# A fused diffusion block and state-space block on one core: first stage in written order, operator products on VectorE, their inputs loaded in long runs and turned on TensorE

## The chip, the cores and the metric

The kernel runs on one core of a Trainium2 chip. The metric is the device time of one execution in microseconds (us), and the time of a version is the median of its runs. A core has five engines that run side by side, each through its own row of instructions: TensorE (PE in the profile, with the weight loads as PEld), VectorE (DVE), ScalarE (ACT), GpSimd (POOL) and SyncE (SP), which issues transfers. [...] Engines wait for each other by semaphores.

## The reference

Two blocks run one behind the other on 256 tokens of width 1024, all in float32.

```python
def first_block(x, c, ctx, c_ctx, ada_w, ...):
    silu_c, silu_cc = jax.nn.silu(c), jax.nn.silu(c_ctx)
    for i in range(DEPTH):                                  # 2 layers
        mod_lat = (silu_c @ ada_w[i] + ada_b[i])[:, None, :]     # adaLN: 1024 x 6144 weights
        mod_ctx = (silu_cc @ ada_w[i] + ada_b[i])[None, None, :]
        sh1, sc1, ga1, sh2, sc2, ga2 = jnp.split(mod_lat, 6, axis=-1)
        ...
        u_lat = modulate(rms_norm(h_lat, g_mix[i]), sh1, sc1)
        u_ctx = modulate(rms_norm(h_ctx, g_mix[i]), csh1, csc1)
        # i == 0: q, k, v of both; neighbourhood attention with a bias; i == 1: sliding window
        ...
        # then h + ga1 * y, and a squared-ReLU MLP of width 4096

def s5_mixer(xn, w_in, lam_re, lam_im, b_re, b_im, c_re, c_im, d_skip, log_dt, w_glu):
    u = (xn @ w_in).astype(f32)
    lam = lax.complex(lam_re, lam_im);  dt = jnp.exp(log_dt)[:, None]
    a_bar = jnp.exp(lam * dt)
    b_bar = ((a_bar - 1.0) / lam)[..., None] * b_mat        # 64 groups, 64 states, 16 inputs
    # scan  s = a_bar * s + b_bar u,  y = Re(c s) + d_skip * u, in chunks
    ...
    val, gate = jnp.split(jax.nn.gelu(y) @ w_glu, 2, axis=-1)
    return val * jax.nn.sigmoid(gate)

def second_block(x, ...):
    # s5_mixer, conv FFN, stick-breaking attention, conv FFN, each with a residual
    ...
```

The operators of the state-space layer hang on weights alone (lambda, dt, b, c, d). The kernel builds them at its very beginning, beside the adaLN work of the first layer, and puts them in DRAM for later.

## The kernel before

Activations lie transposed, in 8 tiles `h[k]` (tokens) and 8 tiles `hc[k]` (context) of 128 x 256: 128 of the 1024 channels by 256 tokens. A product with a weight is done in three passes of a rounded format: the weight is split in `whi` (ScalarE) and a remainder `wlo` (VectorE), the input in `xh` and `xl`, and TensorE adds whi·xh, wlo·xh and whi·xl in one PSUM bank `g` (helper lines 301 to 303, for the first attention layer's projections).

The first stage stands in lines 902 to 988. In it are:

- *Loads.* The condition vectors, the constant table `cst` (with the identity `ident`), the S5 weights (`s5_load`, line 574: `lt` for lambda, `ld` for dt, `bt` for b, `ci` for c, `dr` for d), the tokens and context (`xloads`), and about 20 small vectors (`small_loads`: into `va`, `swg` and, for the attention bias, `rp` and from there to DRAM as `rpad`). All are issued by SyncE through `dma`. `bt` is read with states on the partitions, which makes runs of 64 bytes.
- *adaLN.* 16 steps `ada_step()`, each with 512 KB of `ada_w` (issue in line 354) in buffers `ada` and `stl` and eight matmuls into a bank `x` (line 359). After eight steps the sum goes through `adacc` (a VectorE copy, then a turn on TensorE, line 366) into the modulation vectors `mods` and `scg`. `prep_vectors` turns `va` (line 213) into `vt`, which holds their biases and gains. The first projection needs the modulation of both groups of eight steps, 16 in all.
- *Turns and norm.* x and ctx are transposed on TensorE and copied to `h` and `hc` by ScalarE; `rstd` squares them (ScalarE), sums over channels (TensorE, line 427), takes the reciprocal of the root (VectorE, line 431) and spreads it over the partitions (TensorE, line 438).
- *State-space operators* (class `S5`). The constructor makes the powers of a_bar (`pw`, 0 to 8) and b_bar (`bb`). `c()` turns `ci` on TensorE, has ScalarE copy it to `ct`, and makes `dd` (d on a diagonal, 32 x 1024) on VectorE. For each r in 0 to 3, `e(r, eng)` forms the complex products of powers and b_bar: two tiles `e` from 24 instructions of 128 x 256, 16 products into `tm` and 8 sums or differences into `e`. r = 0 and 1 are on VectorE, 2 and 3 on GpSimd. `k1(r)` multiplies `e` with `cbk` (from ct) and adds dd on TensorE into one bank (lines 722 and 725), copied to `kt`; `et(r)` transposes the e tiles (line 736), which ScalarE copies to `et` and SyncE stores in DRAM as `edr` (line 739); `k2(r)` turns kt into `kst` (line 744). `zero()`, `save()` and `k_out()` store zeros, ct and the powers (`cdr`), and kst (`kdr`, line 759).
- *First projection.* `normed` makes xh and xl from h and hc, and the projections of the first attention layer begin; the heads' attention is worked in pairs, with scores `sc` (line 1106), a bias `bt` loaded from rpad (line 1088), softmax on VectorE and ScalarE, transposes `pt` of the probabilities p (line 850) and p·v into `po` (line 1120).

The order of each engine's instructions is not that of the code: a scheduler of the framework chooses among the instructions that it takes to be ready, by its own model of their costs, over the whole program. In the ordering of the first stage k1 of r = 0 thus falls between adaLN steps, and SyncE's stores of edr among its weight loads. A tile waits for its buffer to come free; a buffer is named by its tag.

Of the kernel before, what the change touches and what calls it, by code (L numbers as in the profile page):

```python
# [16 lines left out]
D = 1024  # L17
KT = 8
# [64 lines left out]
def _build(ctx, tc, I, out, dbg):  # L83
# [3 lines left out]
    dma = nc.sync.dma_start  # L87
# [82 lines left out]
    def vector_loads(va, cc):  # L170
# [31 lines left out]
        return [lambda o=o, i=i: dma(out=o, in_=i) for o, i in todo]  # L202
# [370 lines left out]
    def s5_load(pp):  # L573
# [3 lines left out]
        bt = [spare(i, f"bt{i}").rearrange("p (g h) -> p g h", h=16) for i in range(2)]  # L577
# [5 lines left out]
        for r, nm in ((0, "a_b_re_2"), (1, "a_b_im_2")):  # L583
            todo.append((bt[r], I[nm][0].rearrange("(g j) p h -> (j p) g h", j=2)))
# [4 lines left out]
        return (lt, ld, dr, bt, ci), [lambda o=o, i=i: dma(out=o, in_=i) for o, i in todo]  # L589

    class S5:


        def __init__(self, pp, loads):
# [10 lines left out]
            for i in range(4):  # L605
                T.transpose(pl[:, i * 32:(i + 1) * 32], lt[:, i, :], ident[0:32, 0:32])
            L = pp.tile([128, 128], F32, name="L")
# [23 lines left out]
            self.pw = pw = [pp.tile([128, 9, 32], F32, name=f"pw{i}") for i in range(2)]  # L631
            G.memset(pw[0][:, 0, :], 1.0)
# [17 lines left out]
            tb = [tmp_tile().rearrange("p (g h) -> p g h", h=16) for _ in range(2)]  # L650
            cmul(bb, bt, cb, tb)
# [8 lines left out]
            for r in range(2):  # L660
                act(pf[:, r], pw[r][:, 1:9, :], AF.Copy)
            u = [(cs, sn), (s_[7], s_[8])]
            for i in range(3):
                cmul((ph[:, 0], ph[:, 1]) if i == 2 else u[(i + 1) % 2], u[i % 2], u[i % 2], (t0, t1))

            self.em = [[pp.tile([128, 4, 2, 8, 16], F32, name=f"e{r}{i}") for i in range(2)] for r in range(3)]
            self.tm = [spare(2 + i, f"tm{i}").rearrange("p (i j t h) -> p i j t h", i=2, j=2, t=8) for i in range(2)]
            self.kt = [None] * 4
            self.ci, self.dr = ci, dr

        def c(self):
            pp, ct, ci, dr = self.pp, self.ct, self.ci, self.dr

            for r in range(2):
                for i in range(2):
# [3 lines left out]
                    for j in range(2):  # L679
# [3 lines left out]
            cbs = spare(5, "cbk")  # L683
            G.memset(cbs, 0.0)
            self.cbk = [cbs[:, 256 * i:256 * i + 256].rearrange("p (q a b h) -> p q a b h", q=4, a=2, b=2)
                        for i in range(2)]
# [10 lines left out]
        def save(self):  # L697
            for i in range(2):
                dma(out=cdr[:, 512 * i:512 * i + 512], in_=self.ct[i].rearrange("p g h -> p (g h)"))
# [193 lines left out]
    with ExitStack() as sa:  # L893
# [11 lines left out]
        with ExitStack() as s0:  # L905
# [28 lines left out]
            def some(n):  # L934
                for f in small_loads[0:n]:
                    f()
# [924 lines left out]
```

## Time and profile before

| | before |
|---|---|
| median of 3 runs | 1799.22 us (1796.97 to 1801.13) |
| profiled execution | 1797.98 us, span 1796.3 us |
| TensorE busy | 1712.8 us (95% of the span) |
| VectorE busy | 1177.8 us (66%) |
| ScalarE busy | 795.9 us (44%) |
| GpSimd busy | 468.4 us (26%) |
| mean granted TensorE clock | 0.983 |

The rows are from one profiled execution, the one of 1797.98 us. "Busy" is time in which an instruction runs, issuing of transfers left out. A wait is put down to the instruction whose semaphore came last. Matmul records of one engine overlap, because matmuls are pipelined: the pace of a row of matmuls is seen from their starts and not from their lengths. A float32 matmul is recorded as two passes, a transpose as one.

### The profile page before, as it was taken

How to read it: one execution, taken by the hardware profiler on the slowest of the kernel's cores; microseconds unless marked ns; L12 is line 12 of the kernel's file. 1: busy time of each engine (PE TensorE's matmuls, PEld its weight loads, DVE VectorE, ACT ScalarE, POOL GpSimd, SP SyncE). 2: the span in 40 equal slices, each digit the busy share in tenths (PEclk: the TensorE clock that was granted, in tenths of full speed). 3: DMA queues.
4: the chain of work that ended last, by engine and by line, in shares of the span. 5: the costliest groups of instructions: out<-in, count | busy, mean ns of one | idle time of the engine just before them, and what ended most of it. 6: DMA issues, size and time to landing. Idle time of an engine off the chain costs nothing. (4 is left out here: it accounts for less than half of the span.)

```text
span 1796.3 us, 33733 instructions
## 1 busy us (share of the span) xinstructions
PE 1712.8 (95%) x13161; PEld 1504.6 (84%) x13161; DVE 1177.8 (66%) x2412; ACT 795.9 (44%) x1463; POOL 468.4 (26%) x633
## 2 busy tenths in 40 slices
PE   5899999989999999999998999989999999999999
PEld 3478888867777777888877999978899999789998
DVE  7656887865535343446985656768576788958674
ACT  4354444543413132323674535536444465544443
POOL 5312221125699100030102000221431322424130
PEclk9899999999999999999999999999999999999999
DMA  8565455434666655332216666798459474335852
GB/s 216 178 175 162 138 167 160 109 104 138 199 208 210 192 158 161 93 95 82 72 35 165 177 194 182 222 294 223 129 149 244 141 220 141 107 107 165 230 150 89
DMA packets 441042, 286.57 MB, mean 160 GB/s; under 512 B 50450, under 2 KB 418610, under 8 KB 440882
## 3 DMA queue, kind: packets, MB, share of 16 engines
q1 hardware_dynamic: 439122, 278.64, 53.8%
q0 software_dynamic: 1760, 5.77, 0.8%
q8 instruction: 104, 1.70, 0.4%
q14 instruction: 56, 0.46, 0.1%
HBM read 271.41 MB, written 17.15 MB: 161 GB/s over the span
## 5 line engine op out<-in xcount | busy, mean ns | idle before, releaser
L108 ACT ACTIVATE whi<-raw 128x1024 fp32r<-128x1024 f32 (+2 forms) x388 | 389.7, 1012 | 487.9 <-PE g L294 345.8
L111 DVE TENSOR_TENSOR wlo<-raw,whi 128x1024 fp32r<-128x1024 f32 (+2 forms) x388 | 466.2, 1206 | 186.7 <-ACT whi L108 183.3
L295 PE MATMUL g<-xh,wlo 128*128 128x256 f32 (+1 forms) x1216 | 374.8, 308 | 5.5 <-DVE wlo L111 5.2
L293 PE MATMUL g<-xh,whi 128*128 128x256 f32 (+1 forms) x1216 | 374.8, 309 | 1.2 <-ACT xh L108 1.2
L294 PE MATMUL g<-xl,whi 128*128 128x256 f32 (+1 forms) x1216 | 373.9, 308 | 0.0
L293 PE MATMUL g<-oh,whi 128*128 128x256 f32 (+1 forms) x1056 | 331.5, 315 | 3.5 <-ACT oh L108 1.4
L295 PE MATMUL g<-oh,wlo 128*128 128x256 f32 (+1 forms) x1056 | 331.2, 314 | 0.0
L294 PE MATMUL g<-ol,whi 128*128 128x256 f32 (+1 forms) x1056 | 330.9, 313 | 0.0
L295 PEld LDWEIGHTS g<-xh,wlo 128*128 128x128 f32 x1216 | 234.6, 193 | 17.9 <-DVE wlo L111 7.4
L293 PEld LDWEIGHTS g<-xh,whi 128*128 128x128 f32 x1216 | 234.5, 193 | 16.6 <-ACT whi L108 3.5
L294 PEld LDWEIGHTS g<-xl,whi 128*128 128x128 f32 x1216 | 234.8, 193 | 9.6
L293 PEld LDWEIGHTS g<-oh,whi 128*128 128x128 f32 x1056 | 198.0, 188 | 23.9 <-issue 3.9
L294 PEld LDWEIGHTS g<-ol,whi 128*128 128x128 f32 x1056 | 198.3, 188 | 15.2 <-issue 0.9
L295 PEld LDWEIGHTS g<-oh,wlo 128*128 128x128 f32 x1056 | 198.3, 188 | 14.4 <-issue 0.2
L301 PE MATMUL g<-whi,xh 128*128 128x256 f32 x560 | 167.9, 300 | 3.8 <-ACT xh L108 2.8
L302 PE MATMUL g<-wlo,xh 128*128 128x256 f32 x560 | 161.9, 290 | 0.4 <-DVE wlo L111 0.4
L303 PE MATMUL g<-whi,xl 128*128 128x256 f32 x560 | 160.8, 289 | 0.1
L114 DVE SCALAR_TENSOR_TENSOR h<-g,mods,h 128x256 f32<-128x256 f32 x64 | 30.9, 483 | 140.7 <-PE g L295 140.7
L301 PEld LDWEIGHTS g<-whi,xh 128*128 128x128 f32 x560 | 108.8, 194 | 14.7 <-issue 10.3
L302 PEld LDWEIGHTS g<-wlo,xh 128*128 128x128 f32 x560 | 108.7, 194 | 2.1 <-DVE wlo L111 1.5
L303 PEld LDWEIGHTS g<-whi,xl 128*128 128x128 f32 x560 | 108.1, 194 | 1.1 <-issue 0.6
L108 ACT ACTIVATE oh<-t 128x256 fp32r<-128x256 f32 (+1 forms) x108 | 51.3, 482 | 125.5 <-DVE t L111 125.5
(304 smaller groups left out, 2873.0 us busy)
## 6 DMA issues: line engine op xcount, KB each, us to landing
raw<-mlp_w SPq DMA_DIRECT2D x128, 512.0 KB, 4.4
ada<-ada_w SPq DMA_DIRECT2D x88, 512.0 KB, 6.1
raw<-ffn_w_up SPq DMA_DIRECT2D x88, 512.0 KB, 5.5
raw<-ffn_w_down SPq DMA_DIRECT2D x32, 384.0 KB, 3.8
raw<-ffn_w_down SPq DMA_DIRECT2D x32, 320.0 KB
raw<-na_wqkv SPq DMA_DIRECT2D x32, 256.0 KB, 4.0
raw<-a_w_glu SPq DMA_DIRECT2D x16, 512.0 KB, 7.4
raw<-w_kv SPq DMA_DIRECT2D x16, 512.0 KB, 5.5
```

The costliest lines, as they stand in the source:

```text
L108: last[0] = A.activation(out=o, in_=i, func=f, **kw)
L111: (e or V).tensor_tensor(out=o, in0=a, in1=b, op=op)
L114: V.scalar_tensor_tensor(out=o, in0=a, scalar=s, in1=b, op0=op0, op1=op1)
L293: T.matmul(ps, lhsT=a, rhs=xh[k][:, s0:s1], start=first, stop=False)
L294: T.matmul(ps, lhsT=a, rhs=xl[k][:, s0:s1], start=False, stop=False)
L295: T.matmul(ps, lhsT=b, rhs=xh[k][:, s0:s1], start=False, stop=last_)
L301: T.matmul(ps, lhsT=xh[k][:, t0:t0 + 128], rhs=a, start=first, stop=False)
L302: T.matmul(ps, lhsT=xh[k][:, t0:t0 + 128], rhs=b, start=False, stop=False)
L303: T.matmul(ps, lhsT=xl[k][:, t0:t0 + 128], rhs=a, start=False, stop=last_)
```

## The change

The first stage stands in a `tc.manual_schedule` block for all five engines: there each engine runs the instructions in the order in which the code issues them, up to the operators of r = 1 and the last three adaLN steps. The code of the stage is rewritten in the order meant: S5 constructor, turns of x and ctx, power tables, four adaLN steps, c, e(0), two steps, norm and vectors, three steps, e(1), the operators of r = 0, and so on. Behind the block the scheduler decides again.

The products e(r) are all on VectorE, in 12 instructions of 128 x 512 for each r. For that, GpSimd copies the powers into `pz` (8 copies of 128 x 64) in another order, and b_bar is written in that order. b is loaded in four transfers with runs of 4 KB (32 x 1024 each), and 64 small TensorE operations (32 transposes, 32 float32 matmuls with the identity, 96 passes in all) turn it into two PSUM banks, from where VectorE multiplies it.

The small vector loads, rpad and the four ci loads are issued by GpSimd; the S5 loads besides ci, and the stores of et, ct and the powers, by ScalarE. k1 issues four matmuls that write to four groups of 32 partitions behind one another, and the dd matmuls in two groups of four. The copies of the powers for `pf` come in `c()`. The pool `pp` is allocated from the other side of the memory.

```diff
-        bt = [spare(i, f"bt{i}").rearrange("p (g h) -> p g h", h=16) for i in range(2)]
+        bt = [[pp.tile([128, 1024], F32, tag=f"e{1 + r}{j}", name=f"bt{r}{j}")[0:32] for j in range(2)]
+              for r in range(2)]
...
-            todo.append((bt[r], I[nm][0].rearrange("(g j) p h -> (j p) g h", j=2)))
+            for j in range(2):
+                todo.append((bt[r][j], I[nm][0].rearrange("(g j) p h -> g j (p h)", j=2)[:, j]))
...
-        return (lt, ld, dr, bt, ci), [lambda o=o, i=i: dma(out=o, in_=i) for o, i in todo]
+        return (lt, ld, dr, bt, ci), [
+            lambda o=o, i=i, n=n: (G.dma_start if 7 <= n < 11 else dma_a)(out=o, in_=i) for n, (o, i) in enumerate(todo)]
...
+            pb = [bank("s") for _ in range(2)]
+            for r in range(2):
+                for j in range(2):
+                    b_ = bt[r][j].rearrange("g (p h) -> g h p", h=16)
+                    for h_ in range(16):
+                        o_ = pb[r][64 * j:64 * j + 64, 32 * h_:32 * h_ + 32]
+                        if j:
+                            T.matmul(o_, lhsT=b_[:, h_, :], rhs=ident[0:32, 0:32])
+                        else:
+                            T.transpose(o_, b_[:, h_, :], ident[0:32, 0:32])
...
+            self.pw2 = [pp.tile([128, 32, 8], F32, name=f"pz{i}") for i in range(2)]
+            for i in range(2):
+                for r in range(4):
+                    ts(self.pw2[i][:, 8 * r:8 * r + 8, :].rearrange("p (q j) t -> p q j t", q=4),
+                       pw[i][:, 0:8, :].rearrange("p t (q r j) -> p r q j t", q=4, r=4)[:, r], 1.0, MUL, 0.0, ADD, e=G)
...
-        def e(self, r, eng):
-            em, tm = self.em[r], [self.tm[eng is G][:, i] for i in range(2)]
...
-            for q in range(4):
-                cmul([x_[:, q] for x_ in em], [x_[:, q].unsqueeze(3).to_broadcast([128, 2, 8, 16]) for x_ in pa],
-                     [x_[:, q].unsqueeze(2).to_broadcast([128, 2, 8, 16]) for x_ in ma], tm, e=eng)
+        def e(self, r):
+            for hf in range(2):
+                g = slice(8 * r + 4 * hf, 8 * r + 4 * hf + 4)
+                cmul([x_.rearrange("p q j t h -> p (q j) t h")[:, 4 * hf:4 * hf + 4] for x_ in self.em[r]],
+                     [x_[:, g, :].unsqueeze(3).to_broadcast([128, 4, 8, 16]) for x_ in self.pw2],
+                     [x_[:, g, :].unsqueeze(2).to_broadcast([128, 4, 8, 16]) for x_ in self.bb], self.tm)
...
-            for q in range(4):
-                for jp in range(2):
-                    for i in range(2):
+            for jp in range(2):
+                for i in range(2):
+                    for q in range(4):
                         T.matmul(kp[32 * q:32 * q + 32, jp * 128:(jp + 1) * 128],
...
+                for q in range(4):
                     T.matmul(kp[32 * q:32 * q + 32, jp * 128:jp * 128 + 16], lhsT=self.dd[:, 8 * q + 2 * r + jp, :],
...
-                dma(out=edr[:, 16 * q + 4 * r:16 * q + 4 * r + 4, :], in_=et)
+                dma_a(out=edr[:, 16 * q + 4 * r:16 * q + 4 * r + 4, :], in_=et)
...
-            s5.e(0, V)
-            s5.e(2, G)
...
+            with tc.manual_schedule(engines={ENG.PE, ENG.DVE, ENG.Activation, ENG.SP, ENG.Pool}):
+                for f in vloads[0:2] + [lambda: dma(out=cst, in_=I["cst"])] + sloads[0:7] + xloads + small_loads[0:15]:
+                    f()
+                prep_cond(cc, sc)
+                s5 = S5(pp, loads)
...
+                s5.tables()
...
+                ada(4)
+                s5.c()
+                s5.e(0)
+                ada(2)
+                act(small, h[KT - 2][:, 0:1], AF.Sqrt, bias=eps, scale=0.0)
+                r_ = rstd(512, 0, None, "s")
+                prep_vectors(va)
+                ada(3)
+                s5.e(1)
+                operators(0)
+                ada(2)
+                w_first = [Weights(wpairs(w, D, 0), by_k=True)]
+                ada(2)
+                s5.e(2)
+                small_loads[-1]()
...
+                operators(1)
+                ada(3)
+            w_first.append(Weights(wcols(w, 2 * D, 256), by_k=True))
+            x = new_x(xa, "x", 512)
+            normed(x, r_, 512, lambda k, v: scg[0][:, 0, k, v:v + 1], lambda k, v: modcol(0, 0, k, v))
+            operators(2)
+            s5.e(3)
+            operators(3)
```

How this moves instructions is seen in the row of each engine. On TensorE, behind the spread of the reciprocal root, before the change (`e_268` and `e_269` are the two e tiles of r = 0):

```order
L438 MATMUL s<-sd,cst 128x128 x4
L359 MATMUL x<-ada,sl 32x256 x4
L722 MATMUL s<-e_268,cbk 32x128
L722 MATMUL s<-e_269,cbk 32x128
L736 MATMUL s<-cst,e_268 128x128 x2
L725 MATMUL s<-cst,dd 32x16
L722 MATMUL s<-e_268,cbk 32x128
L722 MATMUL s<-e_269,cbk 32x128
L213 MATMUL x<-cst,va 128x128
L725 MATMUL s<-cst,dd 32x16
```

and after it (`e_426` and `e_427` are the same two tiles):

```order
L367 MATMUL x<-cst,adacc 128x128 x2
L360 MATMUL x<-ada,sl 32x256 x4
L751 MATMUL s<-e_426,cbk 32x128 x4
L751 MATMUL s<-e_427,cbk 32x128 x4
L755 MATMUL s<-cst,dd 32x16 x4
L751 MATMUL s<-e_426,cbk 32x128 x4
L751 MATMUL s<-e_427,cbk 32x128 x4
L755 MATMUL s<-cst,dd 32x16 x4
L766 MATMUL s<-cst,e_426 128x128 x2
```

k1 of r = 0 now comes behind the first adaLN accumulator and in one piece, with four matmuls of one shape behind one another, where pieces of other steps stood among the matmuls before.

On VectorE, at the end of the first products, before the change:

```order
L111 TENSOR_TENSOR tm_274<-pw_200,bb_221 128x256
L431 RECIPROCAL sd<-sd 128x128
L111 TENSOR_TENSOR e_268<-tm_274 128x256
L111 TENSOR_TENSOR tm_274<-pw_199,bb_221 128x256
L111 TENSOR_TENSOR tm_274<-pw_200,bb_220 128x256
L111 TENSOR_TENSOR dd<-dr,cst 32x1024
L111 TENSOR_TENSOR e_269<-tm_274 128x256
```

and after it, at their beginning (`ph` is the last of the power tables):

```order
L112 TENSOR_TENSOR ph<-sm 128x32
L112 TENSOR_TENSOR dd<-dr,cst 32x1024
L112 TENSOR_TENSOR tm_432<-pz_398,bb_309 128x512
L112 TENSOR_TENSOR tm_433<-pz_399,bb_310 128x512
L112 TENSOR_TENSOR e_426<-tm_432,tm_433 128x512
```

dd has moved from among the last products of r = 0 to ahead of the first.

On TensorE, at the first pair of attention heads (`q_1300`, and after it `q_1335`, is the query of that pair), before the change:

```order
L359 MATMUL x<-ada,sl 32x256 x4
L1106 MATMUL sc<-a_1307,q_1300 128x256
L1106 MATMUL sc<-b_1314,q_1300 128x256
L1106 MATMUL sc<-a_1328,q_1300 128x256
L850 MATMUL pt<-cst,p 128x128
L301 MATMUL g<-whi,xh_724 128x256
L359 MATMUL x<-ada,sl 32x256 x2
L302 MATMUL g<-wlo,xh_724 128x256
```

and after it:

```order
L360 MATMUL x<-ada,sl 32x256 x4
L880 MATMUL pt<-cst,p 128x128 x4
L1142 MATMUL sc<-a_1342,q_1335 128x256
L1142 MATMUL sc<-b_1349,q_1335 128x256
L1142 MATMUL sc<-a_1363,q_1335 128x256
L1142 MATMUL sc<-b_1370,q_1335 128x256
L880 MATMUL pt<-cst,p 128x128 x4
L1156 MATMUL po<-pT,vv 64x128 x8
```

Projection matmuls (301, 302) stood between the scores and transposes of this pair; in the changed kernel the projections of the next pair come ahead of it.

## Rows read from the trace of the kernel before

**Rows 1.** Windows: us, busy PE, PEld, DVE, ACT, POOL, PEclk, DMA share, GB/s.

```profile
0.00:80.00 80.00, 50.46 (x385) 28.76 (x385) 55.29 (x140) 29.97 (x81) 38.48 (x58) 0.90 0.68 192
...
128.00:136.00 8.00, 5.75 (x32) 3.60 (x31) 5.09 (x8) 4.44 (x7) 2.74 (x2) 0.79 0.85 234
```

**Rows 2.** Waits of SyncE's queue in 0 to 110 us: total us, times, longest.

```profile
SPq L354 <- PE x L359: 27.5, 4, 11.8
SPq L739 <- ACT et L108: 17.2, 8, 7.0
```

**Rows 3.** Timeline before the first projection: start us, length us, engine, operation, [idle before].

```profile
74.24 0.70 PE L359 MATMUL x<-ada,sl 128*32 128x256 f32 x8 [2.17 <-DMA ada<-ada_w]
...
76.80 0.42 DVE L124 COPY adacc<-x 128x256 f32<-128x256 f32 x1 [7.83 <-PE x L359]
...
79.56 0.98 PE L301 MATMUL g<-whi,xh 128*128 128x256 f32 x2 [1.60 <-ACT xh L108]
```

**Rows 4.** Lines of DVE, 0 to 80 us: busy us, mean ns | idle before.

```profile
L111 DVE TENSOR_TENSOR tm<-pw,bb 128x256 f32<-128x256 f32 x32 | 24.2, 794 | 0.5
L111 DVE TENSOR_TENSOR e<-tm 128x256 f32<-128x256 f32 x16 | 11.1, 691 | 0.4
...
L111 DVE TENSOR_TENSOR wlo<-raw,whi 128x1024 fp32r<-128x1024 f32 x1 | 1.2, 1218 | 0.0
```

**Rows 5.** Lines of POOL, 0 to 80 us.

```profile
L111 POOL TENSOR_TENSOR tm<-pw,bb 128x256 f32<-128x256 f32 x32 | 24.4, 781 | 20.3 <-DVE pw L111 19.1
```

**Rows 6.** Timeline of all engines, 14 to 64 us, single steps of the first stage.

```profile
15.48 1.29 DVE L111 TENSOR_TENSOR t<-bt,sm 128x512 f32<-128x512 f32 x2
...
24.22 0.40 ACT L108 ACTIVATE t<-h 128x256 f32<-128x256 f32 x1
...
28.77 1.57 ACT L108 ACTIVATE ct<-s 64x256 f32<-64x256 f32 x4 [0.16 <-PE s L678]
...
36.95 0.94 DVE L431 RECIPROCAL sd<-sd 128x128 f32<-128x128 f32 x1
...
38.03 2.05 PE L438 MATMUL s<-sd,cst 128*128 128x128 f32 x8 [5.33 <-DVE sd L431]
...
40.09 1.74 DVE L111 TENSOR_TENSOR dd<-dr,cst 32x1024 f32<-32x1024 f32 x1
...
61.37 0.76 DVE L111 TENSOR_TENSOR tm<-pw,bb 128x256 f32<-128x256 f32 x2
```

**Rows 7.** Lines of PE, 79.5 to 110 us.

```profile
L722 PE MATMUL s<-e,cbk 128*32 128x128 f32 x64 | 10.1, 278 | 0.2 <-ACT et L108 0.2
...
L736 PE MATMUL s<-cst,e 128*128 128x128 f32 x40 | 6.7, 306 | 0.0
...
L744 PE MATMUL s<-cst,kt 128*128 128x128 f32 x6 | 1.2, 289 | 0.0
```

**Rows 8.** Timeline of TensorE and its weight loads, operator work among the projections.

```profile
85.55 0.60 PE L722 MATMUL s<-e,cbk 128*32 128x128 f32 x4
...
86.07 0.13 PEld L725 LDWEIGHTS s<-cst,dd 32*32 32x32 f32 x2 [0.20 <-issue]
...
91.23 0.39 PE L303 MATMUL g<-whi,xl 128*128 128x256 f32 x1
...
105.22 1.18 PE L736 MATMUL s<-cst,e 128*128 128x128 f32 x8
...
106.16 0.36 PE L303 MATMUL g<-whi,xl 128*128 128x256 f32 x1
```

**Rows 9.** Timeline of PE, first scores.

```profile
127.62 0.28 PE L1106 MATMUL sc<-a,q 128*128 128x256 f32 x1
...
131.72 0.38 PE L1106 MATMUL sc<-a,q 128*128 128x256 f32 x1 [1.87 <-ACT p L108]
```

**Rows 10.** GpSimd's transfers into fdr: ns min/median/max; landing.

```profile
L814 POOL DMA_DIRECT2D fdr<-fm x16: 710/714/722, 492.9 to 592.2; - x16
...
DMA to landing us min/median/max: 2.4/3.8/6.5
```

## What the change will do to the time: a prediction

> **What bounds the kernel now.** I began with the engine summary of the page: TensorE is busy for 95% of the span, so a change pays only where TensorE stands idle, runs slowly or does less. The window table shows where that is [rows 1]: in the first 80 us TensorE is busy for 50.46 us, at a granted clock of 0.90, against VectorE 55.29 and GpSimd 38.48. This lead-in is no TensorE stage. The timeline gives its end: the first projection matmul of the first attention layer starts at 79.56 [rows 3]. Read backwards from there: the matmul waited for a normalised input, that for the modulation vectors, those for the adaLN accumulator copied at 76.80, and VectorE had then sat idle for 7.83 us waiting for the last adaLN matmuls. These had waited 2.17 us for the weights. So the last adaLN transfer is what ends last, not arithmetic. The SyncE waits say why it is late [rows 2]: 27.5 us of waiting for adaLN buffers to come free, and 17.2 us in which the queue was blocked behind operator stores whose tile ScalarE had not yet copied. Transfers that were ready stood behind stores that were not.
>
> After 79.56 TensorE is nearly always busy, but part of that is the state-space operator work [rows 7], fitted between the projections. I take everything after the first scores as unchanged except for the first attention pairs, since the instruction rows of TensorE agree from the end of the first layer on.
>
> **Term A: the start of the projections.** The new first stage runs in written order on all five engines, so I walked its longest chain. (1) The h copies end in before when ScalarE starts the squares, at 24.22 [rows 6]; the x loads now stand ahead of the S5 loads, so that is an upper end and 21 a lower one. (2) ScalarE then copies ct twice (1.57 for a group of four, so 3.1), copies pf, issues two stores and copies dr, together some 1.5 to 2.5 as an estimate from the 0.39 of one ct piece; VectorE makes dd in 1.74. From 24.2 that ends at 24.2 + 3.1 + 2 + 1.7 = 31. The written order puts dd ahead of the first products, so it now gates them; in before dd fell among the products and gated nothing. (3) Turning b on TensorE is 96 passes; at the 0.118 of an operator transpose (eight from 105.22 to 106.16 [rows 8]) it costs 11.3 us, at half that 6. It follows the lambda transposes at about 9, so it ends by 15 to 20, where before multiplied b at 15.48 [rows 6]. With some 5 us of small VectorE work behind it, bb is there by 25: dd covers it, with 6 us to spare. If dd were early, this would be the gate. (4) The products. In before VectorE does 48 in 24.2 + 11.1 = 35.3 us and GpSimd the other 48 beside it [rows 4, 5]. A shared product is 0.794 there; two behind one another, after GpSimd had finished, take 0.76, so 0.38 each [rows 6]. The 128x512 form was run in 1.29 for two, 0.645 each. So one r is 12 x 0.645 = 7.7 us on VectorE alone, all four 31 us: moving GpSimd's half over costs VectorE no time, it gives back 4 us.
>
> The Trainium skill, page "SBUF — State Buffer", section "Who interferes with whom", says that a VectorE operation with two SBUF inputs contends with GpSimd's reads on a shared port pair. The 794 and 380 ns of this trace agree. By that rule splitting these products buys next to nothing, and a sum that charges GpSimd's 24.4 us to VectorE would be wrong by about as much.
>
> (5) So e(0) ends at 31 + 7.7 = 39. The reciprocal (0.94), the spread on TensorE (2.05) [rows 6] and the vector turn with the first modulations, some 3 to 5, bring e(1) to 45 and its end to 53. Four weight remainders at 1.218 [rows 4] make 4.9, e(2) 7.7: 65.5, with a microsecond either way. (6) From the adaLN accumulator's copy to the first matmul before took 79.56 - 76.80 = 2.8 [rows 3]. TensorE however has the operator work of r = 2 ahead of it now, 3.3 for k1 and 1.9 for the transposes (below), plus about 2 for the copies that these wait for. 65.5 + 7.2 + 2.8 = 75.5; I take 76, so A = 76 - 79.6 = -3.6. Bounds: 70 if the operator work is done while VectorE is busy, 84 if the transfers come one after another as before and the chain only then begins. I take 76 since the sum is of durations in the rows and the SyncE block of 17.2 us is gone: the stores are issued by ScalarE now. These 16 issues, and 12 loads, lie on ScalarE, which is busy for 29.97 of the 80 us.
>
> **Term B: operator work behind the start.** From 79.5 to 110 TensorE ran 64 records of k1, 40 transposes of et and 6 of k2 [rows 7]. A k1 is 32 such records, so two were left, each about 5.7 us (85.55 to 91.23 [rows 8]); with 40 x 0.118 = 4.7 and 6 x 0.12 = 0.7 that is 11.4 + 5.4 = 16.8 us, all on TensorE's path. After, r = 2 stands ahead of the projections and only r = 3 is left. Its k1 no longer changes tile size twice in each of eight groups, but four times in all. One change costs 0.20, the idle time before the small weight load [rows 8]; 12 fewer give 5.7 - 2.4 = 3.3. Not seen in any row is whether four column groups side by side are quicker still; bounds 2.6 and 5.7. Left: 3.3 + 16 x 0.118 + 4 x 0.12 = 5.7. B = 5.7 - 16.8 = -11.1, at worst -8.7.
>
> **Term C: the first attention pairs.** In before projections of pair 1 stand between the scores of pair 0. In the new order they come earlier, and pair 0's chains stand in one block. Such a chain is long: from its score at 127.62 to the matmul that waited for ScalarE's p at 131.72 is 4.1 us, of which 1.87 were idle [rows 9], and the window 128 to 136 has TensorE idle for 8 - 5.75 = 2.25 at a clock of 0.79 [rows 1]. Chains overlap, and VectorE limits them. I take twice that window's loss for the block, +4; bounds -2 (fill found in adaLN steps) and +20 (below).
>
> **Edits at nothing.** The small vector loads and ci go to GpSimd's queue: 0.714 an issue [rows 10], 19 of them 13.6 us, landing 3.8 after; so ci by 19, needed at 24, 5 us of cover. GpSimd has nothing else before the pz copies. The four stores of cdr on ScalarE stand behind other copies with nobody waiting. The right side for the pool changes addresses alone.
>
> **Sum.** -3.6 - 11.1 + 4 = -10.7. The profiled execution took 1797.98, which makes 1787.3; the median of the runs lies 1.2 higher, so 1788.5.
>
> **The rivals.** (a) No gain: the written order couples five engines, and each late load delays all behind it. If the projections start at 84 to 86 (dd at 40 instead of 31) the -11.1 is given back, A = +5 to +6.5 with C = +4: -1, about 1798. For it: nothing in a written order is filled when its head waits. Against: the head's steps are all in the rows. (b) Slower, attention runs dry: eight chains of 4.1 us one behind another are 33 us, with 12 us of TensorE work in them, so C = +20 and the sum +5.3: 1804.5. It decides from C = 14.7. For it: the 1.87 us idle while a fill was there. Against: the first chain bore a table load, and scores of the next chains do not depend on it. (c) Slower, the GpSimd list is late. If transfers on that queue go one after another, 19 x 3.8 = 72 us, ci lands near 80, dd at 90 instead of 31, and even with 20 us of it hidden under adaLN work the end is near 1828. It decides when a load takes more than 0.714 + (5 + 10.7)/19 = 1.54 us. Against: 16 issues of 710 to 722 ns, landing in 6.5 at the most [rows 10].
>
> The same page of the Trainium skill warns, in section "SBUF: two separate sides", that a DMA issued from GpSimd can starve for descriptors while VectorE runs an operation in a two-port mode. No row shows it; were it so here, (c) would be the case.
>
> (d) More gain: the start at 70 and C at zero, 1799.2 - 9.6 - 11.1 = 1778.5 and below.
>
> **How the numbers follow.** About 0.2%, 3.6 us, is what a measurement of this kernel can tell from no change. Forecast, 1779 to 1795.5: 0.54. (d): 0.10. (a), within 3.6 of 1799.2: 0.17. (b): 0.13. (c): 0.06. So faster 0.64, same 0.17, slower 0.19. The forecast's own range is 1779 to 1795; for 8 in 10 it reaches through (a) and the lower half of (d), to 1776 and 1803.
>
> **What would show it.** Right: the first projection at 74 to 78; dd at 31 and the products at 0.64 each with no gap; SyncE without waits for stores; one k1 behind the start, 3.3 long; TensorE idle by 4 us more around the first scores. Wrong: dd or pz waiting for a load from GpSimd (c), the projections after 82 (a), VectorE or ScalarE named before many scores with over 15 us in all (b). The forecast falls if the transposes of b end after 26, since dd then no longer covers them.

## The result and the profile after

The changed kernel takes 1783.65 us (median of 4 runs, 1778.63 to 1786.28) against 1798.1 us (1796.95 to 1801.13) for the kernel before, run beside it: a ratio of 0.9914, 95% interval 0.9896 to 0.9933, or 14.4 us less. The forecast was 1788.5, and 1776 to 1803 as the range. The profiled execution took 1785.5 us with a span of 1783.8, 12.5 less than the span before.

| | before | after |
|---|---|---|
| span of the profiled execution | 1796.3 | 1783.8 |
| first projection matmul | 79.56 | 76.59 |
| first score of the first attention | 127.62 | 110.65 |
| first output projection of that attention | 361.37 | 344.25 |
| TensorE busy in all | 1712.8 | 1701.6 |

The window table of after (length, busy time and number of instructions of PE, PEld, DVE, ACT and POOL, granted clock, DMA share, GB/s): the lead-in, and the stretch from the start of the projections to the first score. (The first attention pairs stand further down.)

```profile
0.00:80.00 80.00, 57.37 (x583) 41.70 (x584) 56.65 (x144) 42.12 (x104) 19.18 (x44) 0.87 0.82 255
76.50:110.60 34.10, 32.88 (x305) 30.76 (x305) 29.27 (x85) 18.03 (x43) 2.97 (x3) 1.00 0.45 119
```

Against [rows 1] TensorE does 7 us more in the first 80 us and GpSimd half as much, while VectorE's busy time has hardly grown, though all products are its own now (39 of 48 are done by then). From the start of the projections to the first score it takes 34.1 us where it took 48.

How the start is reached, from the timeline of after (start, length, engine, instruction, idle time before it), the rows that answer to [rows 3] and [rows 6]:

```profile
33.14 1.21 DVE L112 TENSOR_TENSOR dd<-dr,cst 32x1024 f32<-32x1024 f32 x1 [2.00 <-ACT dr L109]
34.28 1.27 DVE L112 TENSOR_TENSOR tm<-pz,bb 128x512 f32<-128x512 f32 x2
...
41.76 0.69 DVE L112 TENSOR_TENSOR e<-tm,tm 128x512 f32<-128x512 f32 x1
42.37 0.94 DVE L432 RECIPROCAL sd<-sd 128x128 f32<-128x128 f32 x1
46.18 0.56 DVE L125 COPY vt<-x 128x384 f32<-128x384 f32 x1 [2.87 <-PE x L214]
...
71.34 0.42 DVE L125 COPY adacc<-x 128x256 f32<-128x256 f32 x1
...
73.41 2.70 PE L766 MATMUL s<-cst,e 128*128 128x128 f32 x11
...
76.59 0.39 PE L302 MATMUL g<-whi,xh 128*128 128x256 f32 x1
```

VectorE works without a gap from 34.28 to 43.3, then waits 2.87 us for TensorE, which turns the vectors behind the spread, and three times for about 1 us; it copies the last accumulator at 71.34 with no idle time before it. TensorE's row has transposes and k2 of r = 2 right up to the first projection, and ScalarE's first xh ends at 76.54, so both end there together. TensorE waits for no adaLN weights in these 80 us, where it waited 2.17 before [rows 3].

The products, from the lines of VectorE, 0 to 80 us (mean ns behind the busy time):

```profile
L112 DVE TENSOR_TENSOR tm<-pz,bb 128x512 f32<-128x512 f32 x26 | 16.8, 685 | 0.3
L112 DVE TENSOR_TENSOR e<-tm,tm 128x512 f32<-128x512 f32 x13 | 9.0, 691 | 0.4
```

And TensorE's k1 of r = 3, the only one left behind the start, on the timeline:

```profile
97.48 0.41 PE L751 MATMUL s<-e,cbk 128*32 128x128 f32 x4
...
98.01 0.64 PE L751 MATMUL s<-e,cbk 128*32 128x128 f32 x16
98.58 0.25 PE L755 MATMUL s<-cst,dd 32*32 32x16 f32 x8
98.76 0.66 PE L766 MATMUL s<-cst,e 128*128 128x128 f32 x4
```

Sixteen product records take 98.58 - 98.01 = 0.57 us, eight of dd 0.18: half a k1 in 0.75. In [rows 8] a whole k1 takes eight pieces of 0.71, so half of it 2.84.

Where the 12.5 us lie: from the start of the projections to the first output projection the spans are 281.8 and 267.7 us. With the 3.0 at the start that makes a lead of 17.1 at the output projection. Behind it 4.6 are lost again, 1435.0 against 1439.6 us, in a part where TensorE's order of instructions is the same in both from the first attention's end on.

### The profile page after: what moved, and what is told of

Read it like the earlier page. It is cut to its first block, busy times and chain, and to the rows that moved or that the text cites. A ratio compares the mean times of both kernels' runs of the same rounds, so it can differ in the third digit from the quotient of the medians.

```text
span 1783.8 us, 33896 instructions
## 1 busy us (share of the span) xinstructions
PE 1701.6 (95%) x13257; PEld 1506.2 (84%) x13257; DVE 1177.1 (66%) x2412; ACT 798.1 (45%) x1463; POOL 446.9 (25%) x619
```

## The experiments

All times are medians beside runs of the kernel before on the same chip, whose medians were 1797.27 for the first four experiments, 1797.52 for the next four and 1798.36 for the last four. In brackets behind a ratio stands its 95% interval. "Start" is the first projection matmul in the profiled execution.

**The changed kernel again.** No edit.

> The changed kernel once more, unaltered, as the measure for the other runs of this group. Theory: its lead over the kernel before is made in the first stage and stands at the first output projection, about 17 us; what of it is missing at the end (12.5 us in the profiled execution) was lost to spells of TensorE at half clock in later stages, so this run shows again a lead of 16 to 18 us there, and a total between 1778 and 1787 that goes with the mean granted clock. Rival: the changed order itself costs 3 to 5 us in later stages; then the lead at the end is 12 to 13 us at the same mean clock as before.

Measured: 1781.41 us (1776.89 to 1786.46, 4 runs), start 76.92, lead at the output projection 15.5, just below the 16 to 18 expected, and 12.4 at the end of the profiled execution, at a mean granted clock of 0.981 against 0.983 before. The times of its four executions go with that clock: 1776.89 and 1777.14 at 0.985 and 0.984, 1785.68 and 1786.46 at 0.981. The stretch behind the output projection, 361.3, 344.2, 345.8 and (in the run with b in short runs, below) 347.8 us to the end, for before, after, this run and that one:

```profile
361.30:1796.30 1435.00, 1385.01 (x10398) 1239.93 (x10397) 915.26 (x1631) 632.85 (x1050) 377.61 (x512) 0.99 0.55 159
```

```profile
344.20:1783.80 1439.60, 1388.03 (x10404) 1243.30 (x10403) 916.39 (x1632) 632.13 (x1049) 378.03 (x514) 0.99 0.54 158
```

```profile
345.80:1783.90 1438.10, 1388.16 (x10404) 1242.44 (x10402) 917.23 (x1632) 631.86 (x1049) 383.43 (x514) 0.99 0.54 159
```

```profile
347.80:1780.80 1433.00, 1384.58 (x10404) 1240.13 (x10402) 917.40 (x1632) 631.70 (x1049) 383.23 (x514) 0.99 0.55 159
```

The theory, that what is given back there is the clock and not a price of the new order, is not shown. The four profiled kernels that keep the old first stage (before, and the three variants of it below) take 1432.1 to 1435.0 us there:

```profile
354.70:1786.80 1432.10, 1382.54 (x10397) 1238.07 (x10396) 914.88 (x1630) 633.00 (x1050) 382.72 (x512) 0.99 0.55 159
```

This is the grouped k1 in the kernel before, the shortest. Of the ten with the changed stage nine take 1435.4 to 1439.6, and only the run with b in short runs, at 1433.0, lies among the former. The clock is a part of it at most: with dd behind the products (below) this stretch has 32.0 us at half clock by the clock records of the trace and takes 1436.6, before has 38.8 and takes 1435.0. So the rival, that the new order costs some us in later stages, is not excluded (the means of the two groups differ by 3.3), and the cause is open.

**k1 in its old grouping.** In the changed kernel:

```diff
-            for jp in range(2):
-                for i in range(2):
-                    for q in range(4):
-                        T.matmul(kp[...], lhsT=cbk..., rhs=em...)
-                for q in range(4):
-                    T.matmul(kp[...], lhsT=self.dd..., rhs=C("dm")...)
+            for q in range(4):
+                for jp in range(2):
+                    for i in range(2):
+                        T.matmul(kp[...], lhsT=cbk..., rhs=em...)
+                    T.matmul(kp[...], lhsT=self.dd..., rhs=C("dm")...)
```

> The changed kernel with k1 issued as before (two product matmuls and one dd matmul for each of eight pieces). Theory: the k1 of r = 3, which lies behind the start of the projections, takes 5.7 us again instead of 2.0, +3.7; that of r = 2 lies ahead of the start and is paid if TensorE is the last there, another 0 to 3.7. So 4 to 7 us slower than the changed kernel. Rival: TensorE has room for it (the copies and VectorE set the pace), then within 1.5 us.

Measured: 1796.23 us (1788.68 to 1803.22, 10 runs), ratio to before 0.9987 (0.9971 to 1.0004): nearly the whole gain is gone, 14.8 us against the changed kernel beside it (1781.41), more than twice what was expected. Start 86.92. TensorE's lines from 44 us to the start, first of this kernel, then of the changed one run again:

```profile
L751 PE MATMUL s<-e,cbk 128*32 128x128 f32 x96 | 18.0, 315 | 2.4 <-ACT cbk L109 2.4
...
L754 PE MATMUL s<-cst,dd 32*32 32x16 f32 x48 | 5.9, 197 | 0.0
```

```profile
L751 PE MATMUL s<-e,cbk 128*32 128x128 f32 x96 | 5.9, 334 | 3.1 <-ACT cbk L109 2.3 <-DVE e L112 0.7
...
L755 PE MATMUL s<-cst,dd 32*32 32x16 f32 x48 | 1.6, 199 | 0.0
```

Three k1 stand ahead of the start in the written order, and all three are on the way: 23.9 against 7.5 us of TensorE, with the adaLN steps queued behind each. I had counted only the one of r = 2 there.

**The scheduler decides.** In the changed kernel, `with tc.manual_schedule(...)` replaced by a plain block.

> The changed kernel without the written order: the scheduler decides in the first stage too, all else is as changed. Theory (the written order matters by bringing the products and operators of r = 0 to 2 ahead of the start): the first projection comes 48 matmul instructions earlier in TensorE's row, so more operator work lies behind it; some 4 to 8 us slower than the changed kernel. Rival (what helps is the new queues, the wide products and the grouped k1, whatever the order): within 2 us of the changed kernel.

Measured: 1785.96 us (1782.87 to 1789.08, 4 runs), ratio 0.9929 (0.9909 to 0.9948), which overlaps that of the changed kernel. It is 4.6 us more than the changed kernel beside it and 2.3 more than its first median. The first projection comes at 69.60, earlier than in any other kernel here, but with 64 records of k1 behind it instead of 32. This lies between the theory (4 to 8 us slower) and the rival (within 2) and decides neither: with the new queues, the wide products and the grouped k1 most of the gain is there without the written order, and whether the written order adds a few us is not shown.

```profile
69.60 0.56 PE L302 MATMUL g<-whi,xh 128*128 128x256 f32 x1
```

**Products of r = 1 twice.** In the changed kernel, `s5.e(1)` is called twice.

> The changed kernel with the products of r = 1 computed twice, 12 more VectorE instructions of 128x512, 8.0 us (8 products at 0.645 and 4 sums at 0.69). Theory: VectorE's written order sets the start of the projections, which moves by 6 to 8 us, and the total by as much. Rival: transfers or ScalarE set it; then the start moves by less than 3 us.

Measured: 1790.15 us (1787.66 to 1793.05, 5 runs), ratio 0.9961 (0.9945 to 0.9976), 8.7 more than the changed kernel beside it (1781.41). Start 86.40, 9.8 later.

VectorE's row does set the start: some 8.2 us on it move the start by 9.5 to 9.8 and the total by 8.7. Why the start moves by more than the added work is not shown.

**The grouped k1 alone, in the kernel before.** The same edit as above in the other direction.

> The kernel before with one part of the change alone: k1 issues four product matmuls behind one another for each half, then the four dd matmuls. Theory: TensorE's time for a k1 falls from 5.7 to 2.0 us; two lie behind the start of the projections there and those ahead of it are hidden by the wait for the last adaLN weights, so 2 x 3.7 = 7.4 us faster than before, about 1790. Rival (the grouping alone makes the whole gain, since undoing it in the changed kernel cost all of it): 14 to 16 us faster, about 1782.

Measured: 1789.46 us (1785.44 to 1791.15, 4 runs), ratio 0.9953 (0.9938 to 0.9968): 8.1 us faster, where 7.4 was expected. The start stays, at 79.66. TensorE's lines from 79.5 to 120, which answer to [rows 7]:

```profile
L722 PE MATMUL s<-e,cbk 128*32 128x128 f32 x64 | 2.8, 280 | 0.2 <-ACT et L108 0.2
...
L726 PE MATMUL s<-cst,dd 32*32 32x16 f32 x32 | 1.0, 188 | 0.0
```

**Products shared again, in the wide form.** In the changed kernel r = 2 and 3 go to GpSimd with temporaries of their own:

```diff
                 s5.e(0)
+                s5.e(2, G)
+                s5.e(3, G)
...
-                s5.e(2)
...
-            s5.e(3)
```

> The changed kernel with the products of r = 2 and 3 (in the wide form, 128x512) on GpSimd, issued behind those of r = 0, VectorE keeping r = 0 and 1. Theory (the two engines take turns on these operands): a VectorE product grows from 0.645 to some 1.3 us while GpSimd works, GpSimd's take about as long, so VectorE's 7.7 us for r = 1 become some 12 to 16, which gives back the 7.7 of r = 2; the start of the projections and the total stay within 3 us of the changed kernel. Rival (VectorE is freed of 7.7 us, which sets the start): 5 to 8 us faster than the changed kernel.

Measured: 1799.57 us (1797.39 to 1806.09, 10 runs), ratio 1.0018 (1.0008 to 1.0028): all of the gain is lost and a little more. Start 85.70. The lines of VectorE (30 to 90 us) and of GpSimd (30 to 100 us):

```profile
L112 DVE TENSOR_TENSOR tm<-pz,bb 128x512 f32<-128x512 f32 x16 | 19.6, 1262 | 0.2
L112 DVE TENSOR_TENSOR e<-tm,tm 128x512 f32<-128x512 f32 x8 | 10.8, 1350 | 0.3
```

```profile
L112 POOL TENSOR_TENSOR tg<-pz,bb 128x512 f32<-128x512 f32 x16 | 22.5, 1424 | 0.6
L112 POOL TENSOR_TENSOR e<-tg,tg 128x512 f32<-128x512 f32 x8 | 12.1, 1513 | 0.6
```

The price was as expected, 1262 ns a product (a mean that takes in some after GpSimd had finished) against 685 alone. The sum was not: I had let the loss on r = 1 be made good by the missing r = 2, and left out that r = 0 slows as well, whose end (52.5 against 42.4 us) holds up the reciprocal and with it TensorE. The start accounts for 9 of the 16 us or so that are lost; another 6.5 lie in the first attention, where scores wait 8.8 us for p against 2.9, 8.0 of it at once, for a reason that was not tested. The two times of a product agree with the rule of the Trainium skill, page "SBUF — State Buffer", section "Who interferes with whom", that a VectorE operation with two SBUF inputs contends with GpSimd's reads.

**Stores on SyncE.** In the changed kernel the `dma_a` of the et, ct and power stores becomes `dma`.

> The changed kernel with the stores of et, ct and the powers issued by SyncE again, in the same written order. Theory: SyncE then waits for ScalarE's copies with the adaLN and projection weights behind it, as in the kernel before (17.2 us of such waits there); the last adaLN weights arrive late and the projections start 3 to 8 us later, the total by 2 to 8 us. Rival (weights have slack in the new order, since what sets the start is TensorE's and VectorE's row): within 1.5 us.

Measured: 1800.69 us (1795.11 to 1803.09, 10 runs), ratio 1.0009 (0.9996 to 1.0022), start 90.46: all of the gain is lost, more than twice the upper end of what was expected. SyncE's longest waits (total us, times, longest), and the one of TensorE that follows from them:

```profile
SPq L769 <- ACT et L109: 30.4, 6, 20.1
```

```profile
PE x L360 <- DMA stl<-ada_w: 6.9, 2, 3.8
```

In a written row a store that waits for ScalarE holds every load behind it, here for 20.1 us at once. TensorE's waits for weights are 8.4 us in all (6.9, and 1.5 for the other buffer), so they are a part of the 13.9 by which the start is later; the rest is not told apart.

**Small loads on SyncE.** In the changed kernel the small vectors, the bias table and the four loads of c are issued by `dma` instead of `G.dma_start`.

> The changed kernel with the small vector loads, the bias table and the four loads of c issued by SyncE, in the same written order (behind the tokens and context, ahead of the adaLN weights). Theory: 19 issues of about 0.4 us put the first adaLN weights 8 us later, of which the adaLN buffers make good a part, since TensorE takes the first weights only at 26 us; within 2 us of the changed kernel. Rival (SyncE's row is short of time): 4 to 8 us slower.

Measured: 1794.97 us (1790.38 to 1796.78, 10 runs), ratio 0.9981 (0.9972 to 0.9991), start 88.39: some 12 us slower than the changed kernel, in the rival's direction and beyond its 4 to 8. The first adaLN load on SyncE's timeline, in this kernel and in the changed one, and the waits of TensorE and VectorE of this kernel that follow:

```profile
32.18 0.56 SPq L355 DMA_DIRECT2D ada<-ada_w  x1
```

```profile
11.27 0.44 SPq L355 DMA_DIRECT2D ada<-ada_w  x1
```

```profile
PE x L360 <- DMA ada<-ada_w: 11.5, 2, 10.0
```

```profile
DVE dd L112 <- ACT dr L109: 17.1, 1, 17.1
```

It is 21 us later and not 8: 25 issues stand ahead of the weights where I had counted 19, and between them SyncE waited, 5.6 us ahead of the bias table alone. The turns of c stand behind four adaLN steps in TensorE's row, and dd behind the copies of these turns, so the first weights gate the products.

**dd behind the products of r = 0.** In the changed kernel:

```diff
-            tt(dd, dr.unsqueeze(2)..., ident..., MUL)
...
                 s5.e(0)
+                s5.diag()
```

> The changed kernel with the making of dd on VectorE moved behind the products of r = 0, where the written order had it ahead of them. Theory: VectorE no longer waits 2.0 us for d from ScalarE, so the products of r = 0 begin at about 31 and not at 34.3; the reciprocal waits for TensorE's sums anyway, so of these 3 us about 1 to 2 reach the start of the projections, and the total falls by 1 to 2. Rival: nothing, since TensorE's row ahead of the start ends last; within 0.5 at the start.

Measured: 1777.94 us (1775.89 to 1783.46, 4 runs), ratio 0.9895 (0.9874 to 0.9916), the lowest median of all. Its interval overlaps that of the changed kernel beside it, so that the total falls is likely and not shown; that the start does, is seen in the trace:

```profile
30.62 1.29 DVE L112 TENSOR_TENSOR tm<-pz,bb 128x512 f32<-128x512 f32 x2
...
40.79 0.95 DVE L432 RECIPROCAL sd<-sd 128x128 f32<-128x128 f32 x1 [0.86 <-ACT sd L109]
```

```profile
73.39 0.39 PE L302 MATMUL g<-whi,xh 128*128 128x256 f32 x1
```

The products begin 3.7 us earlier, the reciprocal 1.6, the projections 3.2 to 3.5, more than the 1 to 2 expected.

**b in short runs.** In the changed kernel b is loaded as before and the 64 turns on TensorE are left out.

> The changed kernel with b loaded as before (two transfers with runs of 64 bytes, from ScalarE's queue) and without the 64 small turns on TensorE. Theory (the turns were covered by the wait for d): VectorE gets b by 15 to 18 as before, TensorE is free 9.5 us earlier, so the tokens are turned earlier; but the short runs take DMA time from tokens and weights; the start moves by -4 to +2, the total by the same. Rival (the long runs are what the change lives on): 4 us slower or more.

Measured: 1781.11 us (1775.82 to 1782.48, 4 runs), ratio 0.9902 (0.9882 to 0.9923): no difference from the changed kernel that can be measured. VectorE multiplies b at 21.64 us, with the turns gone, against 17.53 and 20.07 for the two parts (real and imaginary) that it needs first; the start is 80.53, 3.9 later, outside the -4 to +2 expected. In the profiled execution this is won back behind the output projection (1433.0 above). The total shows neither this nor the rival's 4 us, so that the long runs are worth anything in it is not shown. Why VectorE is later is seen in ScalarE's row: issuing the second transfer in short runs holds it for 9.12 us, where two in long runs took 3.54, and its first operation starts at 11.88 and not at 6.76.

```profile
2.67 9.12 ACTq L591 DMA_DIRECT2D bt<-a_b_im  x1
...
21.64 1.28 DVE L112 TENSOR_TENSOR t<-bt,sm 128x512 f32<-128x512 f32 x2
```

**Stores on ScalarE alone, in the kernel before.** The `dma` of the et, ct and power stores becomes ScalarE's.

> The kernel before with only the stores of et, ct and the powers moved to ScalarE's queue. Theory of the prediction (SyncE, blocked 17.2 us by them, holds up the adaLN weights that end the lead-in): the projections start 3 to 6 us earlier, the total falls by 3 to 6. Rival: in SyncE's row those stores stand behind all sixteen adaLN loads, so they hold up only projection weights and the start stays; total within 2 us of before.

Measured: 1795.24 us (1791.09 to 1796.55, 10 runs), ratio 0.9981 (0.9971 to 0.9992). The total falls by 3.1, but not for the reason given: the start moves the other way, to 94.79, with all four k1 and all transposes now ahead of it. At the output projection the two nearly cancel, a lead of 0.7 in the profiled execution; the rest of its lead lies behind, in the stretch that took 1432.1 to 1435.0 us in the kernels with the old stage. SyncE's waits, 0 to 96 us:

```profile
SPq L354 <- DMA edr<-et: 15.3, 4, 5.8
SPq L202 <- DMA edr<-et: 10.5, 1, 10.5
```

SyncE waits for the landing of stores that another engine issued. What ties its loads to them was not tested.

**Grouped k1 and all new queues, in the kernel before.**

> The kernel before with the grouped k1 and with all transfers on the queues of the changed kernel (small vectors, bias table and c on GpSimd, the S5 loads and the stores on ScalarE), the scheduler deciding, products shared by VectorE and GpSimd as before. Theory: the grouped k1 gives its 8 us and the queues 0 to 4 more, since the first adaLN weights are issued earlier: 1785 to 1790. Rival (GpSimd's products keep its queue and its loads waiting for each other, the stores hold up ScalarE): the same as or slower than the grouped k1 alone, 1790 or more.

Measured: 1794.88 us (1790.44 to 1796.44, 10 runs), ratio 0.9974 (0.9960 to 0.9989), start 82.18: 3.5 us faster than before, where the grouped k1 alone gave 8.1. The rival holds: added to the grouped k1, the new queues cost some 4 to 5 us in the old stage. With which other part of the change they are a gain was not tested; the run in which the scheduler decides has them beside the wide products on VectorE alone and b in long runs, and keeps most of the gain.

## Why the prediction was right, and where it was not

The direction and the range held, and the gain is of the size forecast: -10.7 forecast, -14.4 measured. The main terms, an earlier start and less operator work behind it, are what the runs show. That the sum came so near is in part luck: in A two errors cancel, and some 5 us that the sum had not priced in the first attention are nearly balanced by 4.6 lost behind it. Term by term, in the profiled execution:

| term | forecast | measured |
|---|---|---|
| A, start of the projections | -3.6 | -3.0 |
| B, operator work behind it | -11.1 | -13.0 |
| C, first attention (what A and B leave of 17.1) | +4 | -1.1 |
| behind the attention | 0 | +4.6 |
| sum | -10.7 | -12.5 |

**A came out by luck, by two errors that cancel.** The chain on VectorE was later at each step: dd ended at 34.35 and not 31, since the h copies ended at 27 and not by 24.2 (TensorE began to turn the tokens only at 19.96, behind the 96 passes for b, which the sum had placed beside them) and dd then waited 2.00 more for ScalarE; e(1) began at 49.4 and not 45; the last accumulator was copied at 71.34 and not 65.5. The last leg made it good: from that copy to the first projection took 5.25 us where the sum had 7.2 + 2.8 one behind the other: 12 of the 32 products of k1 of r = 2 and 5 of its 16 transposes were done before it, and the rest ran beside VectorE's modulations. One reason given for A was wrong: the 17.2 us of store waits [rows 2] did not hold up the adaLN weights before, because in SyncE's row of before the loads of all sixteen adaLN steps stand ahead of the first store:

```profile
69.71 0.89 SPq L354 DMA_DIRECT2D stl<-ada_w  x2
...
74.05 3.28 SPq L739 DMA_DIRECT2D edr<-et  x4
```

Moving the stores alone (the kernel before with stores on ScalarE) brought no earlier start. What is left of [rows 2] is the 27.5 us in which SyncE waited for TensorE to free adaLN buffers; what set TensorE's pace there was not tested. In the written order the stores would be in the way, as the run with stores on SyncE shows by +13.9 at the start, and this the sum had not priced.

**The price of the products held.** 685 and 691 ns in the new form against 645 assumed; 8.2 us for one r (four steps of 2.05) against 7.7. That VectorE takes over GpSimd's half at little cost is shown by its busy time, 56.65 us against 55.29, and by the run that gives the half back, with VectorE at nearly twice its time for a product. The 24.4 us put for GpSimd's half are its 32 products alone; its 16 sums took another 12.6. And ScalarE issues 8 loads, not the 12 named there. Neither count enters the sum.

**B was mis-sized in one term.** The k1 of r = 3 took 2.0 us, not 3.3, and less than the lower bound of 2.6. Fewer changes of tile size do not explain that: sixteen records in 0.57 us are 0.036 each, where in the old grouping four records of one column group take 0.52 (85.55 to 86.07 [rows 8]), 0.13 each. So the four column groups, which I had named as not seen in any row and left out of the value taken, run beside each other. The other terms held: 16 transposes 1.6 and two of k2 0.2, so 3.8 in all against the 16.8 of before. The grouping alone is what the grouped k1 in the kernel before shows, 8.1 us for two k1.

**C was half right.** TensorE's idle time from the start of the projections to the output projection grew by the forecast 4 us, from 281.80 - 277.76 = 4.0 to 267.70 - 259.65 = 8.05, in these sums of the window table (seven windows from 79.5 to 361.3, and from 76.5 to 344.2):

```profile
sum 281.80, PE 277.76 PEld 236.22 DVE 207.75 ACT 133.59 POOL 52.29; mean PE 39.68 PEld 33.75 DVE 29.68 ACT 19.09 POOL 7.47
```

```profile
sum 267.70, PE 259.65 PEld 224.26 DVE 207.49 ACT 127.08 POOL 49.66; mean PE 37.09 PEld 32.04 DVE 29.64 ACT 18.15 POOL 7.09
```

The step that failed is that nothing was set against it: some 5 us of other TensorE work went faster, and the sum had no term for that. One part is the granted clock. The windows in which it was below 1.00, two of before and two of after:

```profile
79.50:127.60 48.10, 47.10 (x366) 40.67 (x367) 26.93 (x81) 24.36 (x60) 3.87 (x6) 0.94 0.62 179
127.60:160.00 32.40, 30.15 (x239) 23.68 (x238) 21.82 (x58) 15.54 (x34) 8.95 (x9) 0.95 0.66 194
```

```profile
110.60:144.00 33.40, 30.01 (x251) 25.18 (x252) 23.74 (x75) 14.68 (x40) 8.29 (x12) 0.95 0.61 173
144.00:184.00 40.00, 37.89 (x325) 31.02 (x322) 29.20 (x89) 16.91 (x41) 7.95 (x10) 0.96 0.55 163
```

Length times the missing share makes 4.5 us before and 3.3 after, an estimate, so the clock gives about 1 of the 5. Before, 2.9 of the 4.5 lie at the early projections, which run at half clock (1.2 GHz) up to some 85 us after TensorE had stood idle ahead of the start:

```profile
81.53 0.41 PE L303 MATMUL g<-whi,xl 128*128 128x256 f32 x1
81.75 0.41 PE L301 MATMUL g<-whi,xh 128*128 128x256 f32 x1
```

Such a pair starts 0.22 us apart there, and 0.12 apart after, where a spell at half clock ends at 76.2, just ahead of the start. The other 4 us are seen in the records but not explained. From the start of each to the next, waits left out, the 1152 projection records take 153.3 us before and 149.2 after, the 256 of adaLN 23.1 and 20.8, the 168 of scores 25.4 and 27.0. It is not the operator work among them: in the kernel before with stores on ScalarE none is left behind the start, and the projections still take 153.0.

**The rivals.** (a), no earlier start, did not come, though e(0) ended 3.5 us late; the runs with k1 ungrouped and with stores or small loads on SyncE show that it was near, each with a start of 87 to 90 and a total within 3.2 us of before's. (b) was far off: waits of the scores for p after 110 us are 2.7 us in all, against 1.9 before:

```profile
PE sc L1142 <- ACT p L109: 2.7, 3, 1.9
```

(c) did not come, and was nearer than the sum had it: from 1.45 to 18.0 us GpSimd issued 19 loads at 0.87 each, against the 1.54 from which it decides, and c landed 8 to 10 us after its issue instead of 3.8, which used up the 5 us of cover. TensorE took it at 27.92, without a gap behind four adaLN steps. A load of the list on GpSimd's timeline, and the landing of c (last column, us):

```profile
7.08 0.52 POOL L203 DMA_DIRECT2D va<-ffn_conv_b  x1 [1.41 <-DMA va<-ada_b]
```

```profile
ci<-a_c_re POOLq DMA_DIRECT2D x2, 256.0 KB, 8.0
ci<-a_c_im POOLq DMA_DIRECT2D x2, 256.0 KB, 10.0
```

## What to carry to other kernels

When work is written in a fixed order, price every instruction ahead of the goal on every engine, and price what happens if one of them is late: here five single edits (k1's grouping undone, products on two engines, stores or small loads on the loading queue, one more set of products) each cost some 7 to 18 us, measured against the kernel before beside them, although in the old order k1's grouping alone was worth 8 and the moved stores alone 3. And ask what the fixed order itself is worth: with all else in place, leaving the order to the scheduler cost 2 to 5 us, which these runs can't tell from nothing. A gain of such a change is not a sum of its parts; ask of each part which row it stands in and who is queued behind it. Before moving half of a VectorE job to GpSimd, compare the time of one instruction alone and beside the other engine: if it doubles, the move buys nothing and slows what was on the path.

## What the runs showed of the hardware that was not expected

Matmuls that write four different groups of 32 columns behind one another overlap: 0.036 us a record of 128 moving columns, against 0.13 when records of one group stand behind one another, and 0.71 us for six records when products and dd alternate in size. VectorE and GpSimd, both with two SBUF operands, slow each other: a VectorE product takes 0.69 us alone and 1.26 to 1.35 in the mean beside GpSimd's, and GpSimd's own take 1.42 to 1.51. GpSimd's load issues wait for the landing of earlier ones (1.41 us before the ninth), and its transfers landed after 4.7 to 10 us, in a stretch with a DMA share of 0.90 (0 to 20 us), against a median of 3.8 for the stores in [rows 10]. Issuing a transfer of 256 KB in runs of 64 bytes right behind another held ScalarE's row for 9.12 us (b in short runs). Four executions of one kernel took 1776.89 to 1786.46 us, the longer ones at the lower mean clock (0.981 against 0.984 and 0.985), so a difference of some 5 us between two single executions of a kernel of this length need not lie in the change.
